# Seven products of the feed-forward layer, second half: another order, another queue for the spill stores, another slot rotation

## The chip, the cores and the metric

The kernel runs on one core of a Trainium2 chip. The metric is the device time of one execution in microseconds (us); smaller is better. TensorE (PE in the profile) does the matmuls, VectorE (DVE) and ScalarE (ACT) the elementwise work, GpSimd (POOL) little here, and SyncE (SP) issues the DMAs. Each engine takes its own instructions in order, and waits on semaphores for the others.

## The reference

One layer on 2048 tokens of width 1024 in float32: a combined input projection, a convolution group and a gated linear attention group, an output projection, and then the feed-forward part, which is what this change touches:

```python
mix = jnp.concatenate([conv_out, gla_out], axis=-1) @ w_out[l]
s = layer_norm(DEEPNORM_ALPHA * s + mix, ln1_g[l], ln1_b[l])
f = jnp.square(jax.nn.relu(s @ w_ff1[l])) @ w_ff2[l]
s = layer_norm(DEEPNORM_ALPHA * s + f, ln2_g[l], ln2_b[l])
```

`w_ff1` is 1024 x 4096 and `w_ff2` 4096 x 1024.

## The kernel before

**Precision.** A float32 operand is held as two parts of the matmul's type fp32r, a high and a low one: ACT casts it (L189, the high part), DVE subtracts (L190, the low part). A product of such operands is three matmuls (high x high, high x low, low x high).

**Halves and stages.** The tokens are four subtiles of 512, taken in pairs; the change is in the second pair (the "second half", whose first product starts at 1484.6 us of the span). Both feed-forward matrix products are done by a seven-product scheme (Strassen-Winograd) on 2 x 2 blocks.

**First product, `ff1s_units` (L989).** The 4096 hidden columns are 16 groups `g` of 256. Of each group there are seven products of 12 matmuls of 128x512 (`product`, L1045 to L1049). Their left operands `X[1]` to `X[7]` stay in SBUF; their right operands are sums and differences of the blocks of two raw weight tiles `w1r` (L1011, loads of 512 KB from SP), made by DVE (L1018) and split into a tile `wop`. Raw tiles and `wop` tiles share one ring `wp` of 10 slots. Products 1 and 2 of groups 0 to 9 are done ahead; after that each of these groups takes the other five in the order 6, 7, 5, 4, 3 (`order(g)`, L1041), and groups 10 to 15 take 1, 6, 2, 7, 5, 4, 3.

**Banks.** A product accumulates in a PSUM bank that several share: `a` holds 1, then 1+2; `b` holds 6, then 6+7, then 6+7+4; `c` holds 5, then 5+3. Between two products that share a bank DVE has to read the first state out, so that product 7 waits for a read of `b` (`unit`, L1060 on; `u2` is `a1` plus 6, `u3` is `a1` plus 6+7, then plus 5). Bank `b` is one of two `gl` banks, `a` and `c` are of four `mm` banks. In the trace's names the numbers are left out: `u2` and `u3` are both `u`, `a1` is `a`, `s3` and `s4` are `s`, `h11` is `h`, `p5` is `p`.

**Spill.** After square-of-relu on ACT (L1055, L1056), sums of the four results give the seven left operands of the second product, and `put` (L1051) stores each, 256 KB, to a DRAM tile `hor`. All these stores are issued from SP, in the order of the program, between the loads. For groups 0 to 9 product 1's result is read back (`h11`, L1082).

**Second product, `ff2_units` (L1136).** 28 steps `n`, each four tiles of 12 matmuls (L1235 to L1237). The left operand of step n is `lt[n]` (made from raw tiles `lr`, loads of `hor`), the right one `rt[n]` (from raw weights `wr`). Both take the next of five slots in turn (`op_tile`, L1132): four of a pool `xtp`, in which `X[6]` and `X[4]` lay before, and one `ox` in another pool that opens where the first product's `h2` tiles were, so after their last stores. The turn starts with `lt[0]`, `rt[0]`, and the third, `ox`, is `lt[1]`. For each of the first steps ACT copies the results out of the banks (L1245). Step 0 starts with eight loads of the residual, 512 KB and 256 KB each (`aa`, `ab`, L1223 and L1224), also from SP.

**Order of the work.** The kernel's `Program` emits units with their operand loads ahead as far as the ring of 10 allows, and a framework then orders each engine's instructions; so the order on an engine is not that of the code.

Of the kernel before, what the change touches and what calls it, by code (L numbers as in the profile page):

```python
# [10 lines left out]
F32 = mybir.dt.float32  # L11
# [6 lines left out]
P = 128  # L18
# [20 lines left out]
GP = 4  # L39
# [106 lines left out]
def hymba_kernel(ctx: ExitStack, tc: tile.TileContext, x, meta, ln_in_g, ln_in_b, w_in, small, gate_up,  # L146
# [662 lines left out]
    def open_x(h=False):  # L809
        (B.hs if h else B.ws).close()  # L810
        B.xs, B.x = phase_pool("px", "right")
# [177 lines left out]
    def ff1s_units(half, stats, f2):  # L989
# [49 lines left out]
            return {i: prog.load(op_fn(i)) for i in order(g)}  # L1039

        def order(g):  # L1041
            return (6, 7, 5, 4, 3) if g < NFR else (1, 6, 2, 7, 5, 4, 3)

        def product(ps, sl, i, start):
            for k in range(4):  # L1045
# [2 lines left out]
                nc.tensor.matmul(ps, wh, X[i][:, k, 1, :], start=False, stop=False, skip_group_check=not start)  # L1048
                nc.tensor.matmul(ps, wl, X[i][:, k, 0, :], start=False, stop=(k == 3), skip_group_check=not start)  # L1049

        def put(g, i, t):  # L1051
            nc.sync.dma_start(out=hor[g // GP][i - 1][:, g % GP, :], in_=t)

        def square(t, src):
            nc.scalar.activation(t, src, AF.Relu)  # L1055
            nc.scalar.activation(t, t, AF.Square)  # L1056
# [3 lines left out]
        def unit(g, i, l):  # L1060
            if i in (1, 6, 5):
                bank[{1: "a", 6: "b", 5: "c"}[i]] = gl_tile() if i == 6 else mm_tile()
            ps = bank[{1: "a", 2: "a", 6: "b", 7: "b", 4: "b", 5: "c", 3: "c"}[i]]
            product(ps, prog.slot[l], i, i in (1, 6, 5))
            tt_ = lambda o, x, y, op=ALU.add: nc.vector.tensor_tensor(out=o, in0=x, in1=y, op=op)  # L1065
            st = bank
            if i == 1:
                a1[g] = B.f1.tile([P, SUB], F32, tag="a1", name="a1", bufs=10)
                nc.scalar.copy(a1[g], ps)
            elif i == 2:  # L1070
                h11[g] = B.f1.tile([P, SUB], F32, tag="h11", name="h11", bufs=3)
                square(h11[g], ps)
                put(g, 1, h11[g])
            elif i == 6:
                st["u2"] = B.h.tile([P, SUB], F32, tag="h2", name="u2", bufs=8)
                tt_(st["u2"], a1[g], ps)
            elif i == 7:
                st["u3"] = B.h.tile([P, SUB], F32, tag="h2", name="u3", bufs=8)
                tt_(st["u3"], a1[g], ps)
                if g < NFR:  # L1080
                    h11[g] = B.f1.tile([P, SUB], F32, tag="h11", name="h11", bufs=3)
                    nc.sync.dma_start(out=h11[g], in_=hor[g // GP][0][:, g % GP, :])  # L1082
            elif i == 5:
                tt_(st["u3"], st["u3"], ps)
                square(st["u3"], st["u3"])
                put(g, 4, st["u3"])
            elif i == 4:
                tt_(a1[g], a1[g], ps)
                square(a1[g], a1[g])
                put(g, 2, a1[g])  # L1090
            else:
                a21 = st["u2"]
                tt_(a21, a21, ps)
                square(a21, a21)
                s3 = B.h.tile([P, SUB], F32, tag="h2", name="s3", bufs=8)
                tt_(s3, h11[g], a21, ALU.subtract)
                put(g, 7, s3)
                tt_(a21, a21, st["u3"])
                put(g, 5, a21)
                tt_(h11[g], a21, h11[g], ALU.subtract)  # L1100
                put(g, 6, h11[g])
                s4 = B.h.tile([P, SUB], F32, tag="h2", name="s4", bufs=8)
                tt_(s4, a1[g], h11[g], ALU.subtract)
                put(g, 3, s4)

        def back():
            yield from back_units(half, stats, X)
# [11 lines left out]
        for g in range(NG):  # L1119
            ls = main_loads(g)  # L1120
            for i in order(g):
                if i == 4 and g == NG - 1:
                    ff2_units(half, f2)
                    f2.head()
                prog.add(lambda g=g, i=i, l=ls[i]: unit(g, i, l), [ls[i]], 2.7)
        prog.add(lambda: open_x(True), cost=0.01)
        f2.head2()

    def op_tile(n):
        if n % 5 == 2:  # L1132
            return B.x.tile([P, GP, 2, SUB], F32R, tag="ox", name="ox")
        return xtp.tile([P, GP, 2, SUB], F32R, tag="xt", name="op")

    def ff2_units(half, f2):  # L1136
# [3 lines left out]

        def nxt():
            count[0] += 1
            return op_tile(count[0] - 1)

        stage = {}

# [68 lines left out]
        def start():  # L1215
            for tt in range(TT):
                accs[tt] = a = NS()
                a.c = B.acc.tile([P, 3, 512], F32, tag="c", name="ac", bufs=4)
                a.a = B.acc.tile([P, D], F32, tag="a", name="aa", bufs=4)
                a.b = B.acc.tile([P, D], F32, tag="b", name="ab", bufs=4)  # L1220
                a.slot = {1: a.c[:, 0], 6: a.c[:, 1], 7: a.c[:, 2], 2: a.a[:, :512], 3: a.a[:, 512:],
                          4: a.b[:, :512], 5: a.b[:, 512:]}
                nc.sync.dma_start(out=a.a, in_=s1d[2 * half][tt])  # L1223
                nc.sync.dma_start(out=a.slot[4], in_=s1d[2 * half + 1][tt][:, :512])  # L1224
            fin[half] = accs

        def unit(n, tt):
            q, i = seq[n]
            if tt == 0 and n == 0:
                start()  # L1230
            ps = mm_tile()
            cols = slice(tt * P, (tt + 1) * P)
            for p in range(GP):
# [182 lines left out]
```

## Time and profile before

| | |
|---|---|
| median of 3 runs | 2170.85 us (2165.41 to 2175.27) |
| profiled execution, its own time | 2167.37 us |
| its span | 2165.4 us, mean granted clock 0.988 |
| PE busy | 2068.3 us, 96% |
| DVE busy | 1644.1 us, 76% |
| ACT busy | 965.3 us, 45% |
| chain that ended last | PE 64%, DVE 21%, DMA 6%, issue 4%, ACT 3% |
| first product of the second half, after the products done ahead | 1545.0 to 1824 us |
| second product, second half | from 1824 us on |

Read it so: PE has work in 96% of the span; what is left to look for is the gaps between its matmuls and the stretches in which the granted clock is at its lower level. The profile's own execution lies 3.5 us under the median of the runs.

### The profile page before, as it was taken

The numbers are of one execution on the slowest core, as the hardware profiler recorded it, in microseconds if no ns is written. First come the engines' busy times: TensorE is split into PE (matmuls) and PEld (weight loads), VectorE is DVE, ScalarE is ACT, GpSimd is POOL, SyncE is SP. The second block draws the span as 40 slices with busy tenths as digits, with TensorE's granted clock in tenths as the row PEclk, the third lists the DMA queues.
The fourth block names the chain that finished last, engine by engine and source line by source line (L and its number), as shares of the span: only waits on it lengthen the run. The fifth ranks groups of instructions, "written<-read, shape, count | busy, mean of one in ns | idle before, by whom it ended". The sixth has DMA issues, their size and how long they took to land.

```text
span 2165.4 us, 26574 instructions
## 1 busy us (share of the span) xinstructions
PE 2068.3 (96%) x9336; PEld 1688.3 (78%) x9336; DVE 1644.1 (76%) x2670; ACT 965.3 (45%) x1672; POOL 91.7 (4%) x104
## 2 busy tenths in 40 slices
PE   7999999999999999999999999899988998999995
PEld 5878888878778788888788888778766777788884
DVE  6699899989986644799645567778776665687888
ACT  4553564653633554655422222335533454533332
POOL 2000100000000000000000000011000000000002
PEclk9999999999999999999999999999999999999998
DMA  5533535443455575665887866556454447645421
GB/s 194 178 109 96 160 93 158 127 117 105 124 194 167 188 259 206 219 242 209 318 328 257 295 231 216 163 176 197 135 181 161 156 164 255 241 141 170 136 78 78
DMA packets 211653, 391.04 MB, mean 181 GB/s; under 512 B 19792, under 2 KB 103984, under 8 KB 211520
## 3 DMA queue, kind: packets, MB, share of 16 engines
q1 hardware_dynamic: 211520, 389.36, 53.4%
q8 instruction: 73, 1.20, 0.2%
q14 instruction: 60, 0.49, 0.1%
HBM read 263.21 MB, written 126.07 MB: 180 GB/s over the span
## 4 chain that ended last, share of the span: by engine, by line
PE 64%; DVE 21%; DMA 6%; issue 4%; ACT 3%; POOL 1%; SPq 0%; ACTq 0%; DVEq 0%; POOLq 0%
PE mm L1235 8%; PE mm L1237 8%; PE mm L1236 8%; PE mm L393 7%; PE mm L395 7%; PE mm L394 7%; DVE cacc L729 6%; DMA w1r<-in_w_dram 2%; DVE wsl L190 2%; PE gl L1047 1%; PE gl L1049 1%; PE mm L1047 1%; PE gl L1048 1%; PE mm L1048 1%; PE mm L1049 1%
## 5 line engine op out<-in xcount | busy, mean ns | idle before, releaser
L393 PE MATMUL mm<-xt,wsl 128*128 128x512 f32 x896 | 353.3, 395 | 0.7 <-ACT xt L189 0.7
L395 PE MATMUL mm<-xt,wsl 128*128 128x512 f32 x896 | 351.7, 393 | 0.0
L394 PE MATMUL mm<-xt,wsl 128*128 128x512 f32 x896 | 351.7, 393 | 0.0
L729 DVE SCALAR_TENSOR_TENSOR cacc<-hin,sm,cacc 128x512 f32<-128x512 f32 x480 | 344.2, 745 | 1.6
L189 ACT CAST wsl<-raw 128x512 fp32r<-128x512 f32 x288 | 176.6, 620 | 207.5 <-PE mm L395 55.4
L190 DVE TENSOR_TENSOR wsl<-raw,wsl 128x512 fp32r<-128x512 f32 x284 | 195.0, 694 | 61.4 <-ACT wsl L189 60.8
L1236 PE MATMUL mm<-op 128*128 128x512 f32 x544 | 212.3, 390 | 0.3 <-DVE op L190 0.3
L1235 PE MATMUL mm<-op 128*128 128x512 f32 x544 | 211.9, 390 | 0.3 <-ACT op L189 0.3
L1237 PE MATMUL mm<-op 128*128 128x512 f32 x544 | 212.0, 390 | 0.0
L189 ACT CAST op<-wr 128x1024 fp32r<-128x1024 f32 x92 | 92.4, 1049 | 258.6 <-PE mm L1237 171.7
L393 PEld LDWEIGHTS mm<-xt,wsl 128*128 128x128 f32 x896 | 169.1, 189 | 34.8 <-ACT xt L189 0.9
L394 PEld LDWEIGHTS mm<-xt,wsl 128*128 128x128 f32 x896 | 169.1, 189 | 34.8 <-issue 0.8
L395 PEld LDWEIGHTS mm<-xt,wsl 128*128 128x128 f32 x896 | 168.8, 188 | 34.7
L190 DVE TENSOR_TENSOR op<-wr,op 128x1024 fp32r<-128x1024 f32 x92 | 109.0, 1221 | 40.7 <-ACT op L189 40.3
L1236 PEld LDWEIGHTS mm<-op 128*128 128x128 f32 x544 | 102.1, 188 | 22.1 <-DVE op L190 0.7
L1235 PEld LDWEIGHTS mm<-op 128*128 128x128 f32 x544 | 102.1, 188 | 22.1 <-ACT op L189 0.8
L1237 PEld LDWEIGHTS mm<-op 128*128 128x128 f32 x544 | 102.1, 188 | 21.0
L1235 PE MATMUL mm<-op,ox 128*128 128x512 f32 x192 | 78.9, 411 | 21.1 <-ACT ac L1245 9.4
L190 DVE TENSOR_TENSOR ho<-hr,ho 128x512 fp32r<-128x512 f32 x96 | 64.7, 685 | 34.9 <-ACT ho L189 32.1
L1047 PE MATMUL gl<-x,wop 128*128 128x512 f32 x192 | 78.2, 407 | 13.0 <-DVE u L1065 12.8
L242 POOL TENSOR_TENSOR rs<-rs,nhalf 128x1 f32<-128x1 f32 x46 | 41.8, 908 | 1149.6 <-DVE rs L241 1147.0
L189 ACT CAST wop<-w1r 128x512 fp32r<-128x512 f32 x76 | 46.5, 619 | 94.4 <-DVE w1r L1018 51.0
(299 smaller groups left out, 4328.3 us busy)
## 6 DMA issues: line engine op xcount, KB each, us to landing
hod<-ho SPq DMA_DIRECT2D x112, 512.0 KB, 3.6
op<-hod SPq DMA_DIRECT2D x88, 512.0 KB, 5.7
raw<-in_w_in_dram SPq DMA_DIRECT2D x160, 256.0 KB, 3.0
wr<-in_w_dram SPq DMA_DIRECT2D x64, 512.0 KB, 5.3
lr<-hor SPq DMA_DIRECT2D x52, 512.0 KB, 4.5
raw<-in_w_dram SPq DMA_DIRECT2D x84, 256.0 KB, 2.9
raw<-in_w_out_dram SPq DMA_DIRECT2D x64, 256.0 KB, 3.5
w1r<-in_w_dram SPq DMA_DIRECT2D x32, 512.0 KB, 4.3
```

The costliest lines, as they stand in the source:

```text
L189: nc.scalar.copy(hi, src)
L190: (eng or nc.vector).tensor_tensor(out=lo, in0=src, in1=hi.bitcast(F32), op=ALU.subtract)
L393: nc.tensor.matmul(ps, wh, mov(k, 0), start=(k == 0), stop=False)
L394: nc.tensor.matmul(ps, wh, mov(k, 1), start=False, stop=False)
L395: nc.tensor.matmul(ps, wl, mov(k, 0), start=False, stop=(k == KD - 1))
L729: nc.vector.scalar_tensor_tensor(out=acc, in0=h[:, j:j + SUB], scalar=wc(j), in1=acc, op0=ALU.mult, op1=ALU.add)
L1047: nc.tensor.matmul(ps, wh, X[i][:, k, 0, :], start=start and k == 0, stop=False, skip_group_check=not start)
L1048: nc.tensor.matmul(ps, wh, X[i][:, k, 1, :], start=False, stop=False, skip_group_check=not start)
L1049: nc.tensor.matmul(ps, wl, X[i][:, k, 0, :], start=False, stop=(k == 3), skip_group_check=not start)
L1235: nc.tensor.matmul(ps, lh, rt[n][:, p, 0, :], start=(p == 0), stop=False)
L1236: nc.tensor.matmul(ps, lh, rt[n][:, p, 1, :], start=False, stop=False)
L1237: nc.tensor.matmul(ps, ll, rt[n][:, p, 0, :], start=False, stop=(p == GP - 1))
```

## The change

It does five things, all in the second half.

1. The order of a group's products becomes 6, 5, 7, 3, 4 (and 1, 6, 2, 5, 7, 3, 4 from group 10 on). Product 5's bank is copied out by ACT into `p5` right after it (new line L1083); after product 7 DVE adds bank `b` and `a1` to it; product 4 comes last.
2. The stores of 1, 2 and 4 are issued from ACT's queue instead of SP's (new L1056); those of 3, 5, 6 and 7 stay on SP but are issued one unit later (new L1054).
3. The load of `h11` is issued with product 5 rather than 7 (new L1086).
4. Of the five operand slots of the second product the `ox` slot is taken by every tile with count 4 modulo 5, no longer 2: `lt[2]` is the first to lie there, and `lt[1]` lies in a slot of `xtp`.
5. The eight residual loads are issued at step 2 instead of step 0.

```diff
--- before.py
+++ after.py
@@ -1039,7 +1039,7 @@
             return {i: prog.load(op_fn(i)) for i in order(g)}
 
         def order(g):
-            return (6, 7, 5, 4, 3) if g < NFR else (1, 6, 2, 7, 5, 4, 3)
+            return (6, 5, 7, 3, 4) if g < NFR else (1, 6, 2, 5, 7, 3, 4)
 
         def product(ps, sl, i, start):
             for k in range(4):
@@ -1048,8 +1048,12 @@
                 nc.tensor.matmul(ps, wh, X[i][:, k, 1, :], start=False, stop=False, skip_group_check=not start)
                 nc.tensor.matmul(ps, wl, X[i][:, k, 0, :], start=False, stop=(k == 3), skip_group_check=not start)
 
-        def put(g, i, t):
-            nc.sync.dma_start(out=hor[g // GP][i - 1][:, g % GP, :], in_=t)
+        def put(g, i, t, late=False):
+            o = hor[g // GP][i - 1][:, g % GP, :]
+            if late:
+                prog.defer(1, lambda: nc.sync.dma_start(out=o, in_=t))
+            else:
+                nc.scalar.dma_start(out=o, in_=t)
 
         def square(t, src):
             nc.scalar.activation(t, src, AF.Relu)
@@ -1074,34 +1078,35 @@
             elif i == 6:
                 st["u2"] = B.h.tile([P, SUB], F32, tag="h2", name="u2", bufs=8)
                 tt_(st["u2"], a1[g], ps)
-            elif i == 7:
-                st["u3"] = B.h.tile([P, SUB], F32, tag="h2", name="u3", bufs=8)
-                tt_(st["u3"], a1[g], ps)
+            elif i == 5:
+                st["p5"] = B.h.tile([P, SUB], F32, tag="h2", name="p5", bufs=8)
+                nc.scalar.copy(st["p5"], ps)
                 if g < NFR:
                     h11[g] = B.f1.tile([P, SUB], F32, tag="h11", name="h11", bufs=3)
                     nc.sync.dma_start(out=h11[g], in_=hor[g // GP][0][:, g % GP, :])
-            elif i == 5:
-                tt_(st["u3"], st["u3"], ps)
-                square(st["u3"], st["u3"])
-                put(g, 4, st["u3"])
-            elif i == 4:
-                tt_(a1[g], a1[g], ps)
-                square(a1[g], a1[g])
-                put(g, 2, a1[g])
-            else:
+            elif i == 7:
+                tt_(st["p5"], st["p5"], ps)
+                tt_(st["p5"], st["p5"], a1[g])
+                square(st["p5"], st["p5"])
+                put(g, 4, st["p5"])
+            elif i == 3:
                 a21 = st["u2"]
                 tt_(a21, a21, ps)
                 square(a21, a21)
                 s3 = B.h.tile([P, SUB], F32, tag="h2", name="s3", bufs=8)
                 tt_(s3, h11[g], a21, ALU.subtract)
-                put(g, 7, s3)
-                tt_(a21, a21, st["u3"])
-                put(g, 5, a21)
+                put(g, 7, s3, True)
+                tt_(a21, a21, st["p5"])
+                put(g, 5, a21, True)
                 tt_(h11[g], a21, h11[g], ALU.subtract)
-                put(g, 6, h11[g])
+                put(g, 6, h11[g], True)
+            else:
+                tt_(a1[g], a1[g], ps)
+                square(a1[g], a1[g])
+                put(g, 2, a1[g])
                 s4 = B.h.tile([P, SUB], F32, tag="h2", name="s4", bufs=8)
                 tt_(s4, a1[g], h11[g], ALU.subtract)
-                put(g, 3, s4)
+                put(g, 3, s4, True)
 
         def back():
             yield from back_units(half, stats, X)
@@ -1123,13 +1128,14 @@
                     ff2_units(half, f2)
                     f2.head()
                 prog.add(lambda g=g, i=i, l=ls[i]: unit(g, i, l), [ls[i]], 2.7)
+        prog.add(lambda: None, cost=0.01)
         prog.add(lambda: open_x(True), cost=0.01)
         f2.head2()
 
 
 
-    def op_tile(n):
-        if n % 5 == 2:
+    def op_tile(n, r):
+        if n % 5 == r:
             return B.x.tile([P, GP, 2, SUB], F32R, tag="ox", name="ox")
         return xtp.tile([P, GP, 2, SUB], F32R, tag="xt", name="op")
 
@@ -1140,7 +1146,7 @@
 
         def nxt():
             count[0] += 1
-            return op_tile(count[0] - 1)
+            return op_tile(count[0] - 1, 4 if half else 2)
 
         stage = {}
 
@@ -1220,14 +1226,19 @@
                 a.b = B.acc.tile([P, D], F32, tag="b", name="ab", bufs=4)
                 a.slot = {1: a.c[:, 0], 6: a.c[:, 1], 7: a.c[:, 2], 2: a.a[:, :512], 3: a.a[:, 512:],
                           4: a.b[:, :512], 5: a.b[:, 512:]}
-                nc.sync.dma_start(out=a.a, in_=s1d[2 * half][tt])
-                nc.sync.dma_start(out=a.slot[4], in_=s1d[2 * half + 1][tt][:, :512])
             fin[half] = accs
+
+        def residual(tt):
+            a = accs[tt]
+            nc.sync.dma_start(out=a.a, in_=s1d[2 * half][tt])
+            nc.sync.dma_start(out=a.slot[4], in_=s1d[2 * half + 1][tt][:, :512])
 
         def unit(n, tt):
             q, i = seq[n]
             if tt == 0 and n == 0:
                 start()
+            if n == 2:
+                residual(tt)
             ps = mm_tile()
             cols = slice(tt * P, (tt + 1) * P)
             for p in range(GP):
```

**Where rows move: SP, one group of the first product in steady state.** Names carry the number of the tile; `hor1_6` is the store of left operand 7 of the second product, `hor1_3` that of 4, and so on. Before:

```order
L1011 DMA w1r_13769<-in_w1_dram 128x4x256
L1052 DMA hor1_6_181<-s3_13699 128x512
L1052 DMA hor1_4_179<-u2_13612 128x512
L1052 DMA hor1_5_180<-h11_13631 128x512
L1052 DMA hor1_2_177<-s4_13706 128x512
L1082 DMA h11_13970<-hor1_0_175 128x512
L1052 DMA hor1_3_178<-u3_13742 128x512
L1011 DMA w1r_13880<-in_w1_dram 128x4x256
L1052 DMA hor1_1_176<-a1_12890 128x512
L1011 DMA w1r_13882<-in_w1_dram 128x4x256
```

Now, the group in the same place:

```order
L1054 DMA hor1_6_181<-s3_13799 128x512
L1011 DMA w1r_13870<-in_w1_dram 128x4x256
L1054 DMA hor1_4_179<-u2_13729 128x512
L1054 DMA hor1_5_180<-h11_13751 128x512
L1054 DMA hor1_2_177<-s4_13822 128x512
L1011 DMA w1r_13872<-in_w1_dram 128x4x256
L1086 DMA h11_14093<-hor2_0_182 128x512
L1054 DMA hor1_6_181<-s3_13913 128x512
L1054 DMA hor1_4_179<-u2_13843 128x512
```

The stores of 4 (`hor1_3`) and 2 (`hor1_1`) are gone from between the two raw loads; the first load has moved ahead of the stores of 5, 6 and 3, the second has moved behind them.

**DVE, the same place.** `u2<-a1,gl` is the read of bank `b` that product 7 waits for; `L1018` rows make operands out of the raw tiles of a later group. Before:

```order
L1018 TENSOR_TENSOR s3_13884<-w1r_13880 128x512
L1065 TENSOR_TENSOR s3_13812<-h11_13744,u2_13725 128x512
L1065 TENSOR_TENSOR u2_13725<-u2_13725,u3_13742 128x512
L1065 TENSOR_TENSOR h11_13744<-u2_13725,h11_13744 128x512
L1018 TENSOR_TENSOR w1r_13880<-w1r_13880,w1r_13882 128x4x128
L1065 TENSOR_TENSOR s4_13819<-a1_12890,h11_13744 128x512
L1065 TENSOR_TENSOR u2_13838<-a1_12932,gl_13825 128x512
L1018 TENSOR_TENSOR w1r_13880<-w1r_13880 128x4x128
L1018 TENSOR_TENSOR w1r_13882<-w1r_13882,w1r_13880 128x4x128
L190 TENSOR_TENSOR wop_13888<-w1r_13880,wop_13888 128x4x128
L190 TENSOR_TENSOR wop_13907<-s3_13884,wop_13907 128x4x128
```

Now:

```order
L1069 TENSOR_TENSOR a1_12932<-a1_12932,gl_13830 128x512
L1069 TENSOR_TENSOR s3_13913<-h11_13865,u2_13843 128x512
L190 TENSOR_TENSOR wop_13917<-w1r_13870,wop_13917 128x4x128
L1069 TENSOR_TENSOR u2_13843<-u2_13843,p5_13863 128x512
L190 TENSOR_TENSOR wop_13941<-s3_13891,wop_13941 128x4x128
L1069 TENSOR_TENSOR h11_13865<-u2_13843,h11_13865 128x512
L190 TENSOR_TENSOR wop_13961<-w1r_13872,wop_13961 128x4x128
L1069 TENSOR_TENSOR s4_13936<-a1_12932,h11_13865 128x512
L1069 TENSOR_TENSOR u2_13957<-a1_12977,gl_13944 128x512
L190 TENSOR_TENSOR wop_13981<-w1r_13872,wop_13981 128x4x128
L1018 TENSOR_TENSOR s3_14005<-w1r_13984 128x512
```

The row that first reads a newly loaded raw tile (`s3_13884<-w1r_13880` before, `s3_14005<-w1r_13984` now) stood six rows ahead of the next `u2<-a1,gl`; now it stands two rows behind it.

**ACT, from the first product to the second.** `op` and `ox` with `lr` behind the arrow are casts of left operands; `ac<-mm` copies the banks of step 0. Before:

```order
L1055 ACTIVATE u2_15042<-u2_15042 128x512
L1056 ACTIVATE u2_15042<-u2_15042 128x512
L189 CAST op_15189<-wr_15078 128x2x512
L189 CAST op_15189<-wr_15096 128x2x512
L189 CAST ox_15176<-lr_15105 128x512
L189 CAST ox_15176<-lr_15106 128x512
L189 CAST ox_15176<-lr_15107 128x512
L189 CAST ox_15176<-lr_15108 128x512
L1245 COPY ac_15208<-mm_15228 128x512
```

Now:

```order
L1060 ACTIVATE u2_15057<-u2_15057 128x512
L1059 ACTIVATE a1_15039<-a1_15039 128x512
L189 CAST op_15192<-lr_15147 128x512
L1060 ACTIVATE a1_15039<-a1_15039 128x512
L189 CAST op_15192<-lr_15148 128x512
L1056 DMA hor3_1_190<-a1_15039 128x512
L189 CAST op_15205<-wr_15094 128x2x512
L1256 COPY ac_15224<-mm_15236 128x512
L1256 COPY ac_15227<-mm_15250 128x512
```

`lt[1]` (the casts of `lr_15105` to `lr_15108` before, of `lr_15145` to `lr_15148` now) is an `op` tile and its casts are spread between the last squares.

## Rows read from the trace of the kernel before

**Rows 1.** The page, section 1: busy us, share of the span, instructions.
```profile
PE 2068.3 (96%) x9336; PEld 1688.3 (78%) x9336; DVE 1644.1 (76%) x2670; ACT 965.3 (45%) x1672; POOL 91.7 (4%) x104
```

**Rows 2.** Windows: stretch, its length, busy us (count) of PE, PEld, DVE, ACT, POOL; clock, DMA.
```profile
1545.00:1601.40 56.40, 54.13 (x229) 42.08 (x227) 42.91 (x68) 23.24 (x40) 0.00 (x0) 1.00 0.52 172
1601.40:1690.20 88.80, 75.67 (x310) 58.22 (x310) 59.76 (x93) 34.48 (x56) 0.00 (x0) 0.98 0.50 164
1690.20:1824.40 134.20, 132.71 (x567) 105.61 (x567) 86.24 (x134) 64.40 (x109) 0.00 (x0) 1.00 0.54 181
1618.80:1623.50 4.70, 4.60 (x12) 3.17 (x12) 2.59 (x5) 1.15 (x3) 0.00 (x0) 0.64 0.37 112
...
1835.50:1843.40 7.90, 0.68 (x3) 0.21 (x2) 3.57 (x5) 2.75 (x6) 0.00 (x0) 0.68 0.91 286
1843.40:1848.00 4.60, 4.54 (x11) 3.58 (x12) 1.67 (x2) 3.47 (x6) 0.00 (x0) 0.50 0.87 224
2100.00:2165.00 65.00, 42.11 (x177) 33.89 (x175) 58.75 (x116) 18.20 (x26) 11.25 (x11) 0.85 0.17 65
```

**Rows 3.** Timeline, 1608 to 1625 us: start, duration, engine, line, operation [idle before <-releaser].
```profile
1609.38 0.69 DVE L190 TENSOR_TENSOR wop<-w1r,wop 128x512 fp32r<-128x512 f32 x1
...
1610.10 0.38 SPq L1011 DMA_DIRECT2D w1r<-in_w_dram  x1
...
1611.51 0.38 SPq L1011 DMA_DIRECT2D w1r<-in_w_dram  x1
...
1614.25 0.69 DVE L1018 TENSOR_TENSOR s<-w1r 128x512 f32<-128x512 f32 x1 [2.04 <-DMA w1r<-in_w_dram]
...
1616.15 0.40 PE L1049 MATMUL mm<-x,wop 128*128 128x512 f32 x1
...
1618.12 0.68 DVE L1065 TENSOR_TENSOR u<-a,gl 128x512 f32<-128x512 f32 x1
...
1618.85 0.50 PE L1047 MATMUL gl<-x,wop 128*128 128x512 f32 x1 [2.31 <-DVE u L1065]
...
1624.16 0.50 PE L1047 MATMUL mm<-x,wop 128*128 128x512 f32 x1 [0.71 <-ACT wop L189]
```

**Rows 4.** Waits, 1601.4 to 1690.2 us: engine, line <- releaser: us, times, longest.
```profile
DVE s L1018 <- DMA w1r<-in_w_dram: 10.8, 5, 2.3
PE gl L1047 <- DVE u L1065: 10.3, 6, 2.4
...
PE mm L1047 <- ACT wop L189: 3.5, 5, 0.7
```

**Rows 5.** Waits of SP's DMA queue, 1540 to 1850 us.
```profile
SPq L1052 <- ACT u L1056: 62.6, 15, 7.9
SPq L1052 <- DVE s L1065: 54.5, 30, 4.5
SPq L1011 <- DVE wop L190: 30.8, 14, 5.7
```

**Rows 6.** DMA issues, 1601 to 1690 us: count, KB each, median us to landing.
```profile
w1r<-in_w_dram SPq DMA_DIRECT2D x10, 512.0 KB, 4.6
```

**Rows 7.** Timeline, 1832 to 1848 us, the second product's first two steps.
```profile
1832.16 0.39 PE L1236 MATMUL mm<-op 128*128 128x512 f32 x1
...
1835.47 0.32 SPq L1052 DMA_DIRECT2D hor<-s  x1
...
1835.79 0.39 PE L1237 MATMUL mm<-op 128*128 128x512 f32 x1
...
1840.19 2.17 ACT L189 CAST ox<-lr 128x512 fp32r<-128x512 f32 x4 [9.47 <-DMA hor<-s]
...
1843.46 0.80 PE L1235 MATMUL mm<-op,ox 128*128 128x512 f32 x1 [7.28 <-ACT ac L1245]
...
1844.69 0.46 SPq L1223 DMA_DIRECT2D aa<-s1d  x1
```

**Rows 8.** DMA issues, 1835 to 1860 us.
```profile
lr<-hor SPq DMA_DIRECT2D x8, 512.0 KB, 8.0
```

## The prediction

> **What bounds the kernel now.** I read the page first. PE is busy in 96% of the span [rows 1], so only PE's gaps, and matmuls at the lower clock, can be won. The change begins with the second half's first product, so I cut that part and what follows into windows and compared each with what its matmuls take at the full rate. That rate: 16 matmuls start between 1832.16 and 1835.79 [rows 7], 0.227 us each; a product of 12 is 2.73 us, a group of five 13.65 us. By this measure (count times 0.2275, from the windows' length [rows 2]) the stretch 1545.0 to 1601.4 loses 56.4 - 52.1 = 4.3 us, 1601.4 to 1690.2 loses 88.8 - 70.5 = **18.3 us**, 1690.2 to 1824.4 loses 134.2 - 129.0 = 5.2 us. At the step to the second product PE stops for 7.28 us at 1843.46 [rows 7], and the 11 matmuls after that take 4.6 us at a granted clock of 0.50 [rows 2], the level of 1.2 GHz: 2.1 us more than 11 at the full rate. With some tenths before the stop that is **about 9.7 us**. In 2100 to 2165 DVE is busy for 58.75 of 65 us [rows 2]; the order there does not change, and I count nothing for it.
>
> Then I asked for the waits of the worst stretch: PE waits for DVE's `u` (the read of bank b that product 7 needs) 10.3 us, for a cast on ACT 3.5 us, and DVE waits for a raw tile 10.8 us in 5 times [rows 4]. The timeline shows the chain of one group [rows 3]. The split at 1609.38 ends the use of an old raw tile, SP issues the next load at 1610.10, and it lands 4.1 us later, at 1614.25, where DVE has stood for 2.04 us: the first row that needs the tile is at the head of DVE's queue. From it DVE takes seven instructions, 0.645 us apart, to `u<-a,gl` at 1618.12. PE had its last matmul at 1616.15 and starts product 7 at 1618.85, 2.31 us idle. Twelve matmuls at clock 0.64 follow once (1618.8 to 1623.5 [rows 2]), 2.0 us lost, and 0.71 us for a cast whose slot product 7 sets free. The 310 matmuls of the stretch are five groups of 60 and ten of what follows, so a group loses 18.3 / 5 = 3.66 us and takes 17.3 instead of 13.65: 2.1 in the wait for `u`, 0.7 for the cast [rows 4], 0.4 of clock, and 0.5 of small gaps.
>
> SP is the third witness: its queue stood 62.6 us for squares on ACT, 54.5 us for sums of DVE and 30.8 us for splits [rows 5], each time with whatever came next, raw loads too, behind it.
>
> **The change, part by part.**
>
> *Order of the products and of DVE's rows.* No work goes: DVE has as many instructions as before, ACT gets 16 copies more. What moves is that product 7's predecessor on PE is now product 5, and the read of bank b stands two rows ahead of the first use of a new raw tile instead of six behind. A load that is late now holds up operands two groups ahead, no longer the bank. The read follows only product 6, the sum `s4` and the rows before it. I walked one group by hand from the rows' durations, product 7 starting at 0: 7 ends at 2.9, 3 at 5.4, 4 at 8.1, the rest of 5 at 10.4, 6 at 13.1; after the read of 4's bank at 8.2 DVE has seven rows to the next `u<-a,gl`, which ends between 12.6 and 13.9; the next product 7 starts at 13.7 to 14.1.
>
> *The loads.* The first raw load is now issued at 10.5 of that count and needed at about 15.2; with 4.6 us [rows 6] it lands at 15.1. The second waits on SP behind the store of `s4`. It lands at 13.6 + 4.6 = 18.2 and is needed at 18.2. This closes a loop: second load, its first use on DVE, 14 DVE rows to the next `s4` at 0.645 us (9.0), issue (0.4), load (4.6): **14.0 us** a group, 0.35 above PE's own 13.65. So of 3.66 us a group 3.3 would go, five times, 16.5; less the first group, in which the old queue still runs out, I take **-16 us** of the 18.3; bounds -18.3 (all) and 0 (a new wait as long).
>
> *Start and end of the first product* (losses of 4.3 and 5.2): the same mechanism in small, -2; bounds -6 (most gone) and +3 (the loop's 0.35 us on the four early groups, and a gap where the orders change).
>
> *Copies and stores on ACT.* A copy takes 0.6 us like the other 128x512 rows of ACT; 16 are 10 us. No row of this trace shows a DMA issued from ACT. SP's issue of the same store takes 0.32 us [rows 7]; 48 of them are 15.4 us at that price, at least nothing if they run beside other work. ACT is busy 34.5 of 88.8 us in the worst stretch [rows 2], 6.9 a group, and would have 6.9 + 0.6 + 2 x 0.32 = 8.1 of 13.7. Each such store waits for the square just ahead of it on the same engine, so nothing new is queued behind a wait. I take 0; bounds 0 and +4, if a quarter falls between a cast and its product.
>
> The Trainium skill ("DMA: Bandwidth & Descriptors", section "Issuing engines are not separate DMA queues") says that transfers run on the same 16 engines whichever engine issues them, and that issuing from several saves only the issue time. By that rule alone part two would be worth 48 x 0.32 us of SP's time, and SP is not what PE waits for: nothing. Rows 5 bear against that reading here: the queue was held by waits of 62.6 us in 15 stores, 4.2 us each, not by issues. What the rule would make of the time is the second rival.
>
> *The step to the second product.* `ox` holds `lt[1]` and lies where the last `h2` tiles were. So its casts wait 9.47 us, till 1840.19, for the last store, issued at 1835.47 [rows 7], and the copies that free step 0's banks stand behind them on ACT: PE's 7.28 us. Now `lt[1]` lies in a slot of product 6's operand, dead since that product, and the `ox` tile is first needed 22 us after the last product. What is late next: `rt[1]`, whose raw weights pass SP beside `lr`; I have it ready at 11 to 12 us, needed at 11. The residual, 3 MB from 1844.69 on [rows 7], leaves the stretch in which `lr` took 8.0 us [rows 8] and comes two steps later, needed by the fifth. Of 9.7 us I take **-8.5**; bounds -10 and 0.
>
> *The dummy unit, `h11` with product 5*: the unit holds no instruction; `h11` is loaded groups ahead; 0.
>
> **Sum.** -16 - 2 + 0 - 8.5 = -26.5 us. Against the profiled execution, 2167.4, this gives 2140.9; that execution lies 3.5 us under the median, so against the median of 2170.85 I expect **2144 us**.
>
> **Rivals.**
> 1. *Loads of 6 us.* The loop grows with the load: at 6 us it is 15.4 a group. That loses 1.75 us a group: the middle gains 5 x (3.66 - 1.75) = 9.5, the four early groups, which lose 4.3 / 4 = 1.08 each now, lose 4 x 0.67 = 2.7 more. With -1.5 after 1690 and -8.5: -17, **2154 us**. For it: 8.0 us of `lr` where the engines were full. Against: 4.6 where these loads run, at half the DMA share [rows 2, 6].
> 2. *The queue is worth only its issue time.* Then DVE's waits for raw tiles, 10.8 us, stay and go on to PE by another way, and the middle gains 18.3 - 10.8 = 7.5 less 2 for the late first group: 5.5. With -8.5: -14, **2157 us**. By the rule of the Trainium skill it is this time. Against it: the bank read no longer stands behind the load.
> 3. *The step gains nothing*, since `rt[1]` comes as late as `ox` did: -18, **2153 us**. For it: DMA share 0.91 in the gap [rows 2]; against it: PE waited for copies behind `ox`, and not for a transfer of `rt[1]`.
> 4. *Slower.* The loop through SP decides: the second load sits behind the store of `s4`, which waits for DVE, which waits for the load before. It is worse than before in the middle as soon as 9.4 + load is over 17.3, a load of 7.9 us. At 10 us a group takes 19.4 and loses 5.75; nine groups from 1545 on lose 51.8 instead of 22.6: +29 - 8.5, **2191 us**. Against it: no load of that length in rows 6.
> 5. *It doesn't do what it says*, the order on the engines falling back to the old one: within 0.5%. The listings of the engines' rows speak against it.
>
> **How the numbers follow.** Forecast 0.55, rival 1 0.13, rival 2 0.08, rival 3 0.10, rivals 1 and 3 at once (2162) 0.05, rival 4 0.05, rival 5 or no effect 0.04. About 0.5%, 10.9 us, is what a measurement of this kernel can tell from no change. Faster by more, under 2160: forecast and rivals 1 to 3, 0.86, of which I move 0.03 over for those that land on the edge: 0.83. Slower by more: 0.05 for rival 4. The rest 0.12. The lower end: all of the bounds, -18.3 - 6 - 10 = -34, 2137, less the spread of the runs, 5: 2132. The upper: rivals 1 to 3 with it, 2160. Left out are rivals 4 and 5, the double case and the edges, under 0.2.
>
> **What would show it.** In the changed profile: PE's waits for `u` in front of product 7 gone or under 0.5 us a group, and the pitch of product 7's starts 13.7 to 14.1 us for groups up to 9; SP's waits for ACT's squares gone, the raw loads issued 3 us or more before they are needed, and DVE's wait for them under 0.5 us; ACT's row of `lt[1]` ending before the first product's last matmul plus 2 us, PE's gap there under 2 us and no stretch at clock 0.50 behind it. A pitch of 15 us or more with SP standing at the store of `s4` is rival 1 or 4; a gap of over 5 us at the second product's step 1 is rival 3.

## The result and the profile after

The changed kernel takes 2141.82 us (median of 4 runs, 2136.0 to 2143.11) beside 2170.54 us for the kernel before: ratio 0.9863, 95% interval 0.9834 to 0.9892, so 1.1 to 1.7% faster. A second measurement beside other experiments gave 0.9880 (0.9865 to 0.9894).

The page of the changed kernel, busy time by engine, and the two DMA queues that now carry transfers:

```profile
PE 2061.7 (96%) x9336; PEld 1687.1 (79%) x9336; DVE 1639.6 (77%) x2670; ACT 970.4 (45%) x1688; POOL 92.0 (4%) x104
...
q1 hardware_dynamic: 204608, 376.77, 52.4%
q10 hardware_dynamic: 6912, 12.59, 1.6%
```

PE's share is still 96%: the gain is 24.5 us of span out of 2165, too little for that row. 12.59 MB, the 48 stores, have moved to a queue of their own. Where the time went is seen in the windows (stretch, length, busy us and count of PE, PEld, DVE, ACT, POOL; clock, DMA), cut at the same matmuls as below:

```profile
1547.60:1606.40 58.80, 56.96 (x241) 44.65 (x240) 42.98 (x69) 24.74 (x45) 0.00 (x0) 1.00 0.54 173
1606.40:1677.80 71.40, 70.56 (x302) 55.88 (x301) 56.51 (x90) 34.42 (x61) 0.00 (x0) 1.00 0.61 202
1677.80:1808.80 131.00, 130.33 (x566) 105.55 (x565) 85.93 (x134) 68.74 (x117) 0.00 (x0) 1.00 0.55 191
1808.80:1831.80 23.00, 22.11 (x98) 17.98 (x97) 21.91 (x26) 15.83 (x23) 0.00 (x0) 1.00 0.78 284
2075.00:2140.00 65.00, 42.61 (x176) 34.26 (x174) 58.63 (x116) 18.10 (x26) 11.24 (x11) 0.86 0.17 65
```

The second row answers to the worst stretch of [rows 2]: 302 matmuls in 71.4 us, where before 310 took 88.8, and the clock is 1.00 in every stretch but the end, which is as it was (DVE busy 58.6 of 65 us). The fourth row is the step to the second product, 98 matmuls in 23.0 us with one short wait (0.89 us at 1822.31, for the low part of `rt[1]`).

Since the start of the first product differs from profile to profile (1483.4 to 1491.4 us over all kernels here, with nothing changed ahead of it), I compare stretches between matmuls, from their start times in the timeline. **First product**: from its first to its last matmul start. **Middle**: from its 481st to its 781st. **Step**: from its last to the second product's 97th. Each of these columns comes from one profiled execution. How far two profiles differ with nothing changed in a stretch: e6 repeats the whole change within 1.0, 0.1 and 0.0 us; e3, whose instructions in the first product stand in the order of the kernel before up to its last rows, differs from it by 2.9 and 2.3. Part of that is TensorE's clock, as at 1618.80 in [rows 2], where 0.64 was granted: matmuls that start 0.43 us apart instead of 0.23 cost 1.4 us in the first product of the kernel before (7 of them), 4.3 in e7 (22), 3.7 in e2 (19), 4.3 in e11 (22), and under 1 us in the others.

| kernel (us) | median | ratio (95%) | first product | middle | step |
|---|---|---|---|---|---|
| before | 2170.5, 2168.5 to 2168.8 in the experiments | 1 | 339.0 | 85.8 | 33.2 |
| whole change | 2141.8 | 0.9863 (0.9834, 0.9892) | 322.0 | 71.3 | 23.2 |
| whole change again, e6 | 2142.7 | 0.9880 (0.9865, 0.9894) | 321.0 | 71.4 | 23.2 |
| e1 order only | 2146.6 | 0.9894 (0.9872, 0.9916) | 321.5 | 73.6 | 27.0 |
| e9 only 3 ahead of 4 | 2155.2 | 0.9940 (0.9923, 0.9958) | 330.5 | 77.5 | 28.3 |
| e10 only 5 ahead of 7 | 2160.6 | 0.9957 (0.9942, 0.9972) | 328.8 | 78.1 | 33.1 |
| e2 stores only | 2175.2 | 1.0027 (1.0012, 1.0043) | 344.5 | 80.8 | 34.2 |
| e3 slot turn only | 2156.9 | 0.9941 (0.9919, 0.9963) | 336.1 | 83.5 | 23.5 |
| e5 order and slot turn | 2145.4 | 0.9887 (0.9870, 0.9903) | 321.8 | 73.8 | 29.0 |
| e12 whole, residual early | 2143.2 | 0.9886 (0.9870, 0.9901) | 321.6 | 71.2 | 23.2 |
| e11 whole, 7 ahead of 5 | 2157.0 | 0.9948 (0.9934, 0.9962) | 338.3 | 83.6 | 22.0 |
| e4 whole, store of s4 on ACT too | 2143.7 | 0.9886 (0.9865, 0.9908) | 324.1 | 72.4 | 22.6 |
| e7 first read of bank b on ACT | 2162.0 | 0.9970 (0.9952, 0.9988) | 334.4 | 83.4 | 32.5 |
| e8 raw loads later | 2171.5 (one run) | | 340.9 | 80.4 | 32.5 |

The whole change wins 17.0 us in the first product, 14.5 of them in the middle, and 10.0 at the step. In the 1247 matmuls behind the step, between 290.5 and 292.0 us in every kernel, it wins nothing.

One group of the middle, DVE's timeline of the changed kernel (start, duration, operation, idle before it and who ended it):

```profile
1625.78 0.68 DVE L1069 TENSOR_TENSOR a<-a,gl 128x512 f32<-128x512 f32 x1
...
1628.78 0.68 DVE L1069 TENSOR_TENSOR s<-a,h 128x512 f32<-128x512 f32 x1
1629.39 0.68 DVE L1069 TENSOR_TENSOR u<-a,gl 128x512 f32<-128x512 f32 x1
...
1631.29 0.69 DVE L1018 TENSOR_TENSOR s<-w1r 128x512 f32<-128x512 f32 x1 [0.63 <-DMA w1r<-in_w_dram]
1633.39 0.69 DVE L1069 TENSOR_TENSOR p<-p,gl 128x512 f32<-128x512 f32 x1 [1.41 <-PE gl L1049]
...
1635.63 1.42 DVE L1018 TENSOR_TENSOR w1r<-w1r 128x512 f32<-128x512 f32 x2 [0.82 <-DMA w1r<-in_w_dram]
```

and on PE two starts of product 6 (1626.60 and 1640.89) and the start of product 7 between them (1630.34). The framework lets product 6 of a group run ahead of products 7 and 4 of the group before, so PE goes 7, 3, 4, most of 5, 6, the rest of 5, and 7 again:

```profile
1626.60 0.47 PE L1047 MATMUL gl<-x,wop 128*128 128x512 f32 x1 [0.25 <-DVE a L1069]
...
1630.34 0.40 PE L1047 MATMUL gl<-x,wop 128*128 128x512 f32 x1
...
1640.89 0.47 PE L1047 MATMUL gl<-x,wop 128*128 128x512 f32 x1 [0.18 <-DVE a L1069]
```

Against [rows 3]: product 7 starts without a wait instead of after 2.31 us, and the next one starts at 1644.87, a pitch of 14.5 us (14.1 to 14.9 over the middle). What wait is left stands in front of product 6, 0.2 us: there are two `gl` banks, and it needs the one that product 4 has just left, so it waits for DVE's `a<-a,gl`. DVE still stands for the raw tile, 0.63 us at 1631.29 and 0.82 at 1635.63. The waits of the stretch (us in total, times, longest) answer to [rows 4]:

```profile
DVE w1r L1018 <- DMA w1r<-in_w_dram: 4.5, 5, 1.1
...
DVE s L1018 <- DMA w1r<-in_w_dram: 3.7, 4, 2.2
...
PE gl L1047 <- DVE a L1069: 0.8, 3, 0.4
```

PE's waits are 0.8 us instead of 13.8, DVE's for raw tiles 4.5 + 3.7 = 8.2 instead of 10.8. SP's queue, which answers to [rows 5], stands no less:

```profile
SPq L1054 <- DVE s L1069: 104.3, 31, 11.3
SPq L1011 <- DVE wop L190: 37.6, 6, 10.3
SPq L1086 <- DMA hor<-h: 33.4, 9, 6.1
```

At the step, ACT's timeline has the last cast of `lt[1]` at 1812.84, 4 us after the first product's last matmul, and the first copies of banks right behind:

```profile
1812.84 0.61 ACT L189 CAST op<-lr 128x512 fp32r<-128x512 f32 x1
...
1814.86 1.08 ACT L1256 COPY ac<-mm 128x512 f32<-128x512 f32 x2 [0.39 <-DVE op L190]
```

Before, these casts came at 1840.19 [rows 7], 16.5 us after the last matmul.

### The profile page after: what moved, and what is told of

The parts are those of the page before. It is cut to its first block, busy times and chain, and to the rows that moved or that the text cites. A ratio compares the mean times of both kernels' runs of the same rounds, so it can differ in the third digit from the quotient of the medians.

```text
span 2140.9 us, 26599 instructions
## 1 busy us (share of the span) xinstructions
PE 2061.7 (96%) x9336; PEld 1687.1 (79%) x9336; DVE 1639.6 (77%) x2670; ACT 970.4 (45%) x1688; POOL 92.0 (4%) x104
## 3 DMA queue, kind: packets, MB, share of 16 engines
q10 hardware_dynamic: 6912, 12.59, 1.6%
## 5 line engine op out<-in xcount | busy, mean ns | idle before, releaser
L1246 PEld LDWEIGHTS mm<-op 128*128 128x128 f32 x544 | 102.8, 189 | 28.3 <-issue 6.7
L1251 DVE TENSOR_TENSOR ac<-ac,mm 128x512 f32<-128x512 f32 x72 | 49.1, 683 | 49.3 <-PE mm L1248 49.3
L898 ACT ACTIVATE hr<-mm 128x512 f32<-128x512 f32 x64 | 38.3, 598 | 103.3 <-PE mm L395 103.3
```

Of the source, the lines that this page charges most:

```text
L1246: nc.tensor.matmul(ps, lh, rt[n][:, p, 0, :], start=(p == 0), stop=False)
L1251: add = lambda o, a, b: nc.vector.tensor_tensor(out=o, in0=a, in1=b, op=ALU.add)
```

## The experiments

**Which part is it in the first product? e1, e2.** e1 keeps the order of products (with ACT's copy and the place of the `h11` load) and undoes the rest; e2 keeps the moved stores and undoes the rest:

```diff
# e1, from the changed kernel
-            if late:
-                prog.defer(1, lambda: nc.sync.dma_start(out=o, in_=t))
-            else:
-                nc.scalar.dma_start(out=o, in_=t)
+            nc.sync.dma_start(out=o, in_=t)
-            return op_tile(count[0] - 1, 4 if half else 2)
+            return op_tile(count[0] - 1, 2)
-            if n == 2:
-                residual(tt)
+            if tt == 0 and n == 0:
+                for t_ in range(TT):
+                    residual(t_)
# e2, from the kernel before
-            nc.sync.dma_start(out=hor[g // GP][i - 1][:, g % GP, :], in_=t)
+            if late:                    # stores 3, 5, 6, 7
+                prog.defer(1, lambda: nc.sync.dma_start(out=o, in_=t))
+            else:                       # stores 1, 2, 4
+                nc.scalar.dma_start(out=o, in_=t)
```

> Only the new order of the products with the copy of product 5's bank; stores, slot turn and residual loads as before. Theory O (the middle was won because the bank read no longer stands behind the raw load on DVE): the first product's 1344 matmuls, 339.8 us before and 322.2 us with the whole change, take 323 to 327; the 7.3 us gap at the second product's step 1 stays; about 2156 us. Theory Q (it was won because stores left SP's queue): 334 us or more, 2165 or slower.

> Only the stores moved: 1, 2 and 4 from ACT, 3, 5, 6, 7 one unit later on SP; order, slot turn and residual loads as before. Theory O: the read of bank b still stands five rows behind the first use of the raw tile on DVE, and the first raw load was held by its slot and not by a store, so the first product keeps 336 to 340 us; 2166 to 2172. Theory Q: 323 to 330 us, 2154 to 2160.

e1: 321.5 us, as the whole change. e2: 344.5, 5.5 us slower than before, 2.3 of them at the lower clock, and the time 0.3% longer. The order is all of the gain in the first product; the moved stores give nothing there and cost something in the old order. Theory Q falls. Which half of the move costs it, ACT's queue for three stores or the later issue of the other four, was not tested apart.

**Is it the read's place behind the raw load? e7, e8.** e7 leaves the order alone, but lets ACT copy bank b:

```diff
             elif i == 6:
-                tt_(st["u2"], a1[g], ps)
+                nc.scalar.copy(st["u2"], ps)
+                tt_(st["u2"], a1[g], st["u2"])
```

> The kernel before with one difference: the first read of bank b, for which product 7 waits, is a copy on ACT, and DVE adds a1 to the copy; order of the products as before. Theory O (the read was late because it stands behind the raw load in DVE's queue): the wait in front of product 7 goes, the stretch of matmuls 480 to 780 of the first product takes 71 to 76 us instead of 85.8, and the first product 323 to 330 us. Theory L (the loads and the ring's slots set the pitch, wherever the read stands): 82 to 86 us in that stretch, and 335 us or more.

Theory O falls here too, in the form I had given it: the first product gets 4.6 us of the 17, and the middle stays at 83.4. But part of that is the clock, which in this stretch was 0.94 in the mean and 0.98 before:

```profile
1600.00:1690.00 90.00, 80.74 (x321) 62.47 (x319) 60.80 (x95) 37.35 (x63) 0.00 (x0) 0.94 0.52 172
```

PE's pauses over the first product (what matmul starts lie apart beyond 0.23 us, those at the lower clock left out) are 28.4 us before, 20.7 in e7 and 12.5 in e1: taking the read off DVE removes about half of what the new order removes. The other half has changed hands, as PE's timeline of e7 shows:

```profile
1637.45 0.50 PE L1047 MATMUL mm<-x,wop 128*128 128x512 f32 x1 [1.50 <-ACT wop L189]
...
1638.34 0.50 PE L1047 MATMUL gl<-x,wop 128*128 128x512 f32 x1 [0.16 <-DVE u L1065]
...
1655.43 0.50 PE L1047 MATMUL mm<-x,wop 128*128 128x512 f32 x1 [1.84 <-ACT wop L189]
...
1656.32 0.80 PE L1047 MATMUL gl<-x,wop 128*128 128x512 f32 x1 [0.15 <-DVE u L1065]
```

PE still stands 1.5 to 1.8 us a group, now for a cast, whose operand DVE makes in the same run of rows behind the read. e8 puts a 128 KB load into the same tile ahead of each raw load:

```diff
+                    nc.sync.dma_start(out=t[:, 0:1, :], in_=...)   # the first quarter, again
                     nc.sync.dma_start(out=t, in_=w1[j * 512:(j + 1) * 512, ...
```

> The kernel before, with a small extra load ahead of each raw load into the same tile, so that each raw load lands 2 to 4 us later. Theory O: each microsecond goes into the wait in front of product 7; 2 to 4 us a group more over ten groups, 2185 to 2215 us.

The first product takes 340.9 us, 1.9 more, not 20 to 40. But it is no clean test: the framework put the rows that use the raw tile behind the read of bank b in this kernel, so it also changed the order. The middle takes 80.4 us with loads and order both changed, so it gives no share to either.

**Then the loop of products and DVE: e9, e10, e11.** Reading the kernel before again, with these rows of DVE's and ACT's timelines beside [rows 3]:

```profile
1608.73 0.69 DVE L1065 TENSOR_TENSOR a<-a,gl 128x512 f32<-128x512 f32 x1 [1.43 <-PE gl L1049]
...
1611.52 0.69 DVE L1065 TENSOR_TENSOR u<-u,mm 128x512 f32<-128x512 f32 x1 [1.45 <-PE mm L1049]
...
1612.90 0.63 ACT L1056 ACTIVATE u<-u 128x512 f32<-128x512 f32 x1
```

product 7 starts at 1601.42; 4 and then 3 follow, and 3 ends by 1611.52, 10.1 us later, where DVE has idled for both. Only then can the square of `u2` and the sums run, 7.3 us of ACT and DVE up to product 7 at 1618.85. 10.1 + 7.3 is the pitch of 17.4: products 7, 4, 3 and DVE's rows are a closed chain, in which DVE waits for PE and then PE for DVE. The raw load lies across it, but only briefly: ACT's last square ends at 1613.53, and DVE's run begins at 1614.25 with the load [rows 3], so of the 2.04 us that DVE stands for the load 0.7 are the load's alone. e9 exchanges only 4 and 3, e10 only 7 and 5 (with the copy), each on the kernel before:

```diff
-            return (6, 7, 5, 4, 3) if g < NFR else (1, 6, 2, 7, 5, 4, 3)
+            return (6, 7, 5, 3, 4) if g < NFR else (1, 6, 2, 7, 5, 3, 4)   # e9
+            return (6, 5, 7, 4, 3) if g < NFR else (1, 6, 2, 5, 7, 4, 3)   # e10
```

> The kernel before with products 4 and 3 exchanged and nothing else (order 6, 7, 5, 3, 4). Theory R (the pitch of a group is a closed chain: products 7, 4, 3, then square and seven rows of DVE up to the read of bank b, then product 7 again; 17.4 us): with 3 ahead of 4 its square and two of its sums run beside product 4, the chain falls to 13 to 14.5 us, matmuls 480 to 780 of the first product take 71 to 76 us instead of 85.8, the first product 322 to 328 instead of 339. Theory P (moving product 5 ahead of 7 is what counts): 82 us or more there, 334 or more.

> The kernel before with product 5 ahead of 7, its bank copied by ACT, and 4, 3 last as before (order 6, 5, 7, 4, 3). Theory R: the chain 7, 4, 3, DVE's rows stays closed and only the 0.7 us wait for a cast goes; 80 to 85 us for matmuls 480 to 780, first product 331 to 338 us. Theory P: 71 to 76 us, 322 to 328.

Each gives about half, 8.5 and 10.2 us of the first product, and both exchanges together are e1, 17.5. Neither theory R, which wanted nearly all from e9, nor P, which wanted it from e10, holds alone. What e9 leaves, on PE and on DVE:

```profile
1637.21 0.50 PE L1047 MATMUL gl<-x,wop 128*128 128x512 f32 x1 [0.78 <-DVE u L1065]
```

```profile
1632.62 0.68 DVE L1065 TENSOR_TENSOR u<-a,gl 128x512 f32<-128x512 f32 x1
1636.47 0.69 DVE L1065 TENSOR_TENSOR u<-a,gl 128x512 f32<-128x512 f32 x1 [3.17 <-PE gl L1049]
...
1648.23 0.68 DVE L1065 TENSOR_TENSOR u<-a,gl 128x512 f32<-128x512 f32 x1
```

Behind 7 the framework put half of product 4, of bank b too, so DVE has to read between them: it idles 3.17 us while product 7 runs, then works from 1636.47 to 1648.9 with no gap over 0.35, and PE waits 0.78. 3.2 + 12.4 is the 15.6 us that e9's groups take. In e10 the framework puts 4 or 5 matmuls of product 3 between 7 and 4, and 6 or 7 behind 4. The starts of products 6, 7 and 4:

```profile
1628.46 0.47 PE L1047 MATMUL gl<-x,wop 128*128 128x512 f32 x1 [1.49 <-DVE a L1065]
...
1635.36 0.50 PE L1047 MATMUL gl<-x,wop 128*128 128x512 f32 x1 [0.89 <-DVE u L1065]
...
1640.84 0.50 PE L1047 MATMUL gl<-x,wop 128*128 128x512 f32 x1 [1.26 <-DVE p L1065]
```

PE waits 0.9 to 1.5 us for DVE three times in 14 us, where the whole change has 0.2. In the order 6, 5, 7, 3, 4 every two products of one bank have a product of the other between them, and the long sums hang on the last but one. On PE most of product 5 lies ahead of 7 in the kernel before as well, and 6 is a group ahead; what differs there is the pair 7 and 4 of one bank, with 1 or 2 matmuls of product 5 between them before, none in e9, 4 or 5 of product 3 in e10 and 11 in the whole change. The runs show that the two exchanges give about half each; that it is by way of this pair and the sums is read from the traces. e11 asks whether the second half of that is needed when all else of the change is there (order 6, 7, 5, 3, 4, no copies, stores, slots and residual as changed):

> The whole change, but with product 7 ahead of 5 as before and without ACT's copies (order 6, 7, 5, 3, 4). Theory R: within 0.2% of the whole change, 2139 to 2146 us. Theory P: 2152 us or more.

338.3 us: all but 0.7 us of the gain is lost, and it is 7.8 us slower than e9, about half of that at the lower clock (4.3 us against 0.4). The slot turn and the residual act later, so it is the moved stores that cost time in this order, as in e2, and theory R falls in this form too; the time is in theory P's range, but the moved stores have a part in it, so e11 is no clean answer. e9 beside e1 is the cleaner one. On DVE and PE of e11:

```profile
1617.22 0.68 DVE L1069 TENSOR_TENSOR u<-a,gl 128x512 f32<-128x512 f32 x1
1620.83 2.14 DVE L1018 TENSOR_TENSOR w1r<-w1r 128x512 f32<-128x512 f32 x3 [2.93 <-DMA w1r<-in_w_dram]
```

```profile
1624.03 0.80 PE L1047 MATMUL mm<-x,wop 128*128 128x512 f32 x1 [3.03 <-ACT wop L189]
```

DVE stands 2.93 us for a raw tile and PE 3.03 us after it. Why the loads come later there was not taken further.

**The pitch that is left: e4.** The prediction held the pitch to be closed through SP, by the raw load behind the store of `s4`. e4 takes that store off SP:

```diff
-                put(g, 3, s4, True)
+                put(g, 3, s4)   # from ACT
```

> The whole change, with the store of s4 issued from ACT as well, so that the second raw load no longer stands behind it on SP. If the loop (store of s4, second load, DVE's rows, next s4) sets the pitch of 14.4 us that groups 3 to 8 have with the change: the pitch falls to 13.8 to 14.0 and the time by 3 to 5 us, to 2137 to 2139. If DVE or PE set it: pitch 14.3 to 14.5, time 2141 to 2143.

The middle takes 72.4 us, the pitch of DVE's `h` rows is 14.5 to 14.8, the time 2143.7. The loop through that store doesn't set the pitch. PE's own pitch, 60 starts 0.23 us apart, is 13.8; a good part of the rest is one late read of bank b by DVE in a group, ahead of product 6 in the whole change (0.2 us idle, 0.4 between the starts) and ahead of product 7 in e4 (0.1 to 0.5 idle). Why DVE comes late to it is open.

**The step: e3, e5, e12.** e3 is the slot turn alone on the kernel before (`op_tile(..., 4 if half else 2)`); e5 is e1 with that turn; e12 is the whole change with the residual at step 0.

> Only the turn of the operand slots changed (the third slot group's place taken at count 4 modulo 5). If the slot is the cause of the gap: the second product's first 96 matmuls, 32.4 us before and 23.0 with the whole change, take 23 to 25 us, the 7.3 us gap is gone, 2160 to 2163 us. If the residual loads are as much a cause: 26 to 30 us, 2164 to 2168.

> The new order of the products and the new slot turn, without the moved stores and without the later residual loads. If these two parts are all of the gain: the first product's matmuls take 321 to 324 us from first to last, the second product's first 96 take 22.5 to 24 us, and the time is that of the whole change within 0.2%. If the moved stores or the later residual add to it: 4 us or more above the whole change.

> The whole change, but the eight residual loads at step 0 as before. If the later residual gave the quicker step: the second product's first 96 matmuls with the gap in front of them take 26 to 29 us, as with order and slot turn alone (29.0), instead of 23.2. If the moved stores gave it: 23 to 24.5 us.

> The whole change once more, beside the kernel with two of its parts on the same chip: 2139 to 2145 us.

The slot alone takes the step from 33.2 to 23.5 us, all there is. The order alone takes it to 27.0; its last store leaves 7.7 us after the first product's last matmul, where it was 11.8. Both together take 29.0, no better than the order alone: in e1 and e5 alike PE's first matmul of the second product comes about 3 us late, and behind that e5 has 11 matmuls at the lower clock, e1 5. The later residual does nothing (e12, 23.2). So in the profiles the moved stores are worth 29.0 - 23.2 = 5.8 us here; e5's profile is of the slowest of its four runs, and the medians of e5 and e6, side by side, are 2.8 us apart with intervals that overlap. SP's queue and ACT in e5:

```profile
1799.62 0.34 SPq L1052 DMA_DIRECT2D hor<-h  x1
...
1801.54 3.05 SPq L1155 DMA_DIRECT2D lr<-hor  x6
1808.91 0.32 SPq L1052 DMA_DIRECT2D hor<-p  x1
1809.27 0.94 SPq L1155 DMA_DIRECT2D lr<-hor  x2
```

```profile
1807.72 0.62 ACT L189 CAST op<-lr 128x512 fp32r<-128x512 f32 x1 [1.66 <-DMA lr<-hor]
...
1811.38 1.98 ACT L189 CAST op<-wr 128x1024 fp32r<-128x1024 f32 x2
...
1812.46 1.69 PE L1243 MATMUL mm<-op 128*128 128x512 f32 x4 [3.04 <-ACT op L189]
```

The first `lr` load leaves SP at 1801.54, behind the store of `h`, which waits for its square till 1799.6, and a weight load. Its cast starts at 1807.72 after a wait, the other casts of `lt[0]` and then those of `rt[0]` (1811.38) follow on ACT, and the second product starts 3.4 us after the first's last matmul, at 1812.46. The two `lr` loads behind the store of `p` stand even longer, till 1809.27, but they belong to `lt[1]`. With the stores of `h` and `p` on ACT the first two loads leave SP at 1794.76 and 1797.46, and PE goes on without a gap, at 1808.79:

```profile
1794.76 0.55 SPq L1159 DMA_DIRECT2D lr<-hor  x1
...
1797.46 0.46 SPq L1159 DMA_DIRECT2D lr<-hor  x1
...
1800.26 4.77 SPq L1159 DMA_DIRECT2D lr<-hor  x6
```

The framework also put these loads elsewhere among the weight loads; how much is that and how much the wait for the stores was not separated.

No kernel run here beats the whole change by more than the measurements differ; e4, e6 and e12 lie within 2 us of it.

## Why the prediction was right, and where it was not

**The sum** was -26.5 us. From the first product's first matmul to the end it was 2165.4 - 1484.64 = 680.8 before and 2140.9 - 1486.59 = 654.3 after: -26.5. The medians differ by 28.7; 2144 was forecast, 2141.8 came. So near a hit is partly luck, as the terms show.

**The middle and the ends**, -16 and -2: -14.5 and -2.5. The size is right and its place (the order, with DVE's rows) too; the hand walk's pitch of 13.7 to 14.1 came out as 14.1 to 14.9. What was wrong is the step "the read of bank b stands two rows ahead of the first use of a new raw tile instead of six behind", which I named as what the move does. e7 gives PE that and removes half of the pauses, 4.6 us of the 17 in its profile. "Product 7's predecessor on PE is now product 5" is no change at all: the matmul at 1616.15 in [rows 3], PE's last before product 7, is by its operand product 5's already. The walk held what the exchanges e9 and e10 point to without my naming it: it put product 3 between 7 and 4, and let the sums after product 3 run beside product 4.

**The loads.** "The second waits on SP behind the store of `s4`. This closes a loop": e4 takes the store away and nothing gets faster. Nor did the loads get sooner. I had asked for DVE's wait for raw tiles to fall under 0.5 us a group; from 1545 to 1824 us it rose, 19.2 + 7.1 us before, 20.6 + 13.1 after, and the median load went from 4.6 to 5.5 us. By rival 1's formula a load of 5.5 us would make the pitch 14.9, not 14.5.

**Copies and stores on ACT**, 0: nothing measured speaks against it as a price, though no run has them alone. The copy takes 0.58 us, the store's issue 0.33 us on ACT, as the 0.32 us bound from SP said. But I counted no gain for the stores either, and at the step the profiles show one of 5.8 us beside the new order.

The Trainium skill ("DMA: Bandwidth & Descriptors", section "Issuing engines are not separate DMA queues") has it that issuing from several engines only saves issue time. In the first product e1 against the whole change agrees with what I made of that rule: nothing gained by the other queue. At the step e5's profile differs from it: 5.8 us came with issues of 0.33 us, and SP's queue in e5 is also a line in which loads stand behind stores that wait, till 1799.62 and 1808.91. I had set rows 5 against the rule in the wrong place.

**The step**, -8.5: -10.0. The slot was the cause of the gap, as said, and e3 shows it alone. The share that I gave the residual is nothing (e12). That `rt[1]` might come late instead (rival 3) happened in small: PE waits 0.89 us at 1822.31 for its low part, which DVE makes from 1821.04 on. The sign that I gave for `lt[1]`, its casts done 2 us after the last matmul, missed: they end 4.9 us after it, and PE does not wait for them.

**Rivals.** 2 gave the right cause for the stores and the wrong time, since it let DVE's waits go on to PE; they stayed, and PE did not wait longer for it. 4 fell with e4: no loop through SP, and loads of 5.5 us.

## What to carry to other kernels

Where several products share a bank, look for the closed chain of an engine that waits for PE and PE that waits for it; its length is a floor for the pitch, and taking away the last row in front of PE's stall may free only part of it, here half. Look at the order on PE itself, put a product of another bank between two of one bank that follow each other there, and the product with the longest tail not last. Move a store to another queue where a load that is needed soon stands behind it: the same move was worth 5.8 us in one place (in the profiles), nothing in another, and cost some in a third.

## What was not expected

Parts that are each good need not add up: in the profiles the new order alone wins 6 us of the step and the slot turn alone 10, but both together only 4, until the stores are moved. And moving stores to ACT's queue, or to a later place on SP, made the old order slower (344.5 against 339.0 us, ratio 1.0027, interval 1.0012 to 1.0043).
